# Output projection and the MLP's opening in a hybrid decoder step: matmuls in traced order, norm steps at set units

## The chip, the core and the metric

The kernel runs on one core of one Trainium2 chip. Times are microseconds of device time. The engines are TensorE (PE; its weight loads are PEld), VectorE (DVE), ScalarE (ACT), GpSimd (POOL) and SyncE (SP, which here only issues DMAs). The metric is the time of one execution, the median of several.

## What is computed

One decoder layer for 1024 prompt tokens and 8 single-token samples, 1032 token columns in all, model width 1024, MLP width 2816. The part that the change touches:

```python
def rms_norm(x, g):
    xf = x.astype(jnp.float32)
    y = xf * lax.rsqrt(jnp.mean(xf * xf, axis=-1, keepdims=True) + EPS)
    return (y * g.astype(jnp.float32)).astype(x.dtype)

def conv_ffn(h, buf, w_in, conv_w, conv_b, w_out):
    z = jnp.einsum('btd,df->btf', h, w_in)
    g, u = jnp.split(z, [D_FF], axis=-1)
    xp = jnp.concatenate([buf.astype(g.dtype), g], axis=1)
    c = sum(conv_w[j] * xp[:, j:j + T] for j in range(CONV_W)) + conv_b
    y = jnp.einsum('btf,fd->btd', jax.nn.gelu(c) * u, w_out)
    return y, xp[:, -(CONV_W - 1):]
...
xp = xp + rms_norm(mix_out(ro, rg, do, subln_g[l], lam_i, w_o[l]), norm_mix_post[l])
h = rms_norm(xp, norm_ffn_pre[l])
f, cbuf = conv_ffn(h, ..., w_ffn_in[l], conv_w[l], conv_b[l], w_ffn_out[l])
xp = xp + rms_norm(f, norm_ffn_post[l])
```

Everything is in fp32.

## The kernel before

**Tiling.** Activations lie transposed: 128 channels on the partitions, tokens along the free axis, in three segments s = 0, 1, 2 of 344 tokens (the samples are the last 8 columns of s = 2). An fp32 product is made of three matmuls of rounded parts: high weight by high row, high by low, low by high (`prod3`, lines 112 to 117). High parts are ScalarE copies, low parts VectorE subtractions (`split_w`, line 102). A *unit* is one `prod3` over all eight k: 24 matmuls into one PSUM bank. There are eight banks: two tagged mm, three S, two t, one o.

**Output projection** (line 878). For each s, eight blocks d of 128 output channels. For d = 0, 1 and s = 0, 1 seven of the eight k were multiplied earlier (`first`, line 794), beside the last retention head; only three matmuls are left there. After a unit ScalarE copies the bank, scaled, into `mix` (eight buffers) and squares it into `sq`; POOL adds the squares into `acc`.

**The two norms** (`norms_stage`, line 830) are a generator, one per segment, which the projection and the MLP's opening step forward with `next(chain)`. `rstd_1` sums `acc` over the channels with six small matmuls into `n1` (called n in the rows), then VectorE (`ms`), POOL (`rr`, a power) and VectorE (`rs`, six `dg`) turn it into diagonal matrices; `rstd_2` spreads the factor over the partitions with two matmuls into `bc`. Then the residual is added (`x1`, one buffer, loaded by SP), its squares go into `acc2`, it is stored by ScalarE's queue, and `rstd_1` and `rstd_2` come again; last, `ht` = x1 * gain * bc is split into `hh` and `hl`.

**The MLP's opening** (`ffn_in`, line 921). Blocks j = 0, 1 of the gate and up weights are multiplied directly: for j, s in (0,0), (0,1), (1,0), (1,1) a gate unit (`gp`) and an up unit (`up`) each, then, after line 1006, s = 2 for both j. Each ends with a chain of ScalarE and VectorE steps (convolution, gelu, product) and a store to `ad` or `ad2`.

**Token sums** (line 991). From j = 2 on the segments 0 and 1 are multiplied in Strassen's manner (`block`, line 1056; seven products of half size instead of eight): for each k in 0..3 POOL forms combinations of rows of `hh` + `hl`, and `put` splits them into `tw[0..2]` and over `hh[1]`, `hl[1]`. The first product that reads them is `pb` with `tw[0]` (line 1070).

**Order.** A planner orders the instructions of every engine by its own estimate of when each is ready, and gives buffers as they come free; the order is fixed before the launch, and each engine works through its queue in that order. Under `tc.manual_schedule(engines={PE})` TensorE's instructions keep the order in which they were traced; in the kernel before this holds for the blocks j = 2 to 21 only (lines 1119 to 1126).

**The y stage** (line 1198). `load_t` brings weights and rows by SP's queue; `finish` (line 1135) is a generator that ends a part: factor, then per row of 128 channels a VectorE product, a POOL add into `x1` and a store to `yT` by SP's queue.

Of the kernel before, what the change touches and what calls it, by code (L numbers as in the profile page):

```python
# [18 lines left out]
P = 128  # L19
# [7 lines left out]
ND = D // P  # L27
# [24 lines left out]
def step_kernel(ctx: ExitStack, tc: tile.TileContext, gam, g128, xT, w_in, w_o, w_f, w_y, norms, ngb, cst, subln,  # L52
# [777 lines left out]
    def norms_stage(s, acc, mix):  # L830

        yield
        dg = rstd_1(pw, acc)
        yield
# [5 lines left out]
        for d in range(ND):  # L840
            nc.vector.tensor_tensor(mix[d], mix[d], bc, ALU.mult)
            (nc.vector if d % 2 else nc.gpsimd).tensor_tensor(x1[:, d, :], x1[:, d, :], mix[d], ALU.add)
            add_sq(pw, acc2, x1[:, d, :], d == 0, nc.vector)
            if d % 2:
                yield
        nc.scalar.dma_start(x1d[:, :, s * SEG:(s + 1) * SEG], x1)
        yield
        yield
        yield
        dg = rstd_1(pw, acc2)  # L850
        yield
# [4 lines left out]
        if s == 0:  # L856
            zt = pw.tile([P, ND, 2], F32, name="zt")
            nc.gpsimd.memset(zt, 0.0)
            nc.vector.tensor_copy(a[:, :, 0:2], zt)
            nc.vector.tensor_copy(b[:, :, 0:2], zt)  # L860
        else:
            nc.vector.tensor_copy(a[:, :, 0:2], hh[-1][:, :, SEG:SEG + 2].bitcast(F32))
            nc.vector.tensor_copy(b[:, :, 0:2], hl[-1][:, :, SEG:SEG + 2].bitcast(F32))
        for d in range(ND):
            t = pw.tile([P, SEG], F32, tag="sq", bufs=3, name="ht")
            nc.vector.scalar_tensor_tensor(t, x1[:, d, :], gn[:, 2, d:d + 1], bc, ALU.mult, ALU.mult)
            nc.scalar.activation(a[:, d, 2:SEG + 2], t, AF.Copy)
            nc.vector.tensor_tensor(b[:, d, 2:SEG + 2], t, a[:, d, 2:SEG + 2].bitcast(F32), ALU.subtract)
            if d % 2 and d < ND - 1:
                yield  # L870
        hh.append(a)
        hl.append(b)
        yield

    chain = None
    rot = 0
    w_all = [*w2, split_w(load_w(w_o[2]), wo, "o", bufs=6)]
    for s in range(3):
# [3 lines left out]
        for d in range(ND):  # L882
# [3 lines left out]
            else:  # L886
# [3 lines left out]
                ps = bank(("mm", "S", "S", "mm", "S")[rot % 5], "ps_o")[:, 0:SEG]  # L890
                rot += 1
# [4 lines left out]
            add_sq(pw, acc, ps, d == 0, nc.gpsimd)  # L896
            if chain is not None and (d, s) not in first:
                next(chain, None)
                next(chain, None)
        if chain is not None:  # L900
            for _ in chain:
                pass
        chain = norms_stage(s, acc, mix)
# [64 lines left out]
    for j in range(2):  # L968
        for s in range(2):
            for _ in ffn_in(j, s, *wj[j]):  # L970
                next(chain, None)
                next(chain, None)
    for _ in chain:
        pass
    closed(pw_cm)
# [8 lines left out]
    def part(t, s, k):  # L984
        return t[s][:, k, 2:SEG + 2].bitcast(F32)

# [4 lines left out]
    for k in range(4):  # L991
        b12, b22, t1, t2, t3 = (tt.tile([P, SEG], F32, tag=f"tt{i}", name=f"tt{i}") for i in range(5))
        G = nc.gpsimd.tensor_tensor
        G(b12, part(hh, 1, k), part(hl, 1, k), ALU.add)
        G(b22, part(hh, 1, 4 + k), part(hl, 1, 4 + k), ALU.add)
        G(t3, b22, b12, ALU.subtract)
        put(tw[1][:, 0, k], tw[1][:, 1, k], t3)
        G(t1, b12, part(hh, 0, k), ALU.subtract)
        G(t1, t1, part(hl, 0, k), ALU.subtract)
        G(t2, b22, t1, ALU.subtract)  # L1000
        put(tw[0][:, 0, k], tw[0][:, 1, k], t2)
        G(b12, part(hh, 0, 4 + k), t2, ALU.subtract)
        G(b12, b12, part(hl, 0, 4 + k), ALU.add)
        put(tw[2][:, 0, k], tw[2][:, 1, k], b12)
        put(hh[1][:, k, 2:SEG + 2], hl[1][:, k, 2:SEG + 2], t1)
    closed(t_cm)

# [111 lines left out]
    fixed = tc.manual_schedule(engines={mybir.EngineType.PE})  # L1119
    fixed.__enter__()  # L1120
# [14 lines left out]
    def finish(part, acc, fv, x1):  # L1135
# [6 lines left out]
        for d in range(ND):  # L1142
            nc.vector.tensor_tensor(fv[:, d, :], fv[:, d, :], bs, ALU.mult)
            nc.gpsimd.tensor_tensor(x1[:, d, :], x1[:, d, :], fv[:, d, :], ALU.add)
            nc.sync.dma_start(yT[part, :, d, :], x1[:, d, :])
            yield
# [256 lines left out]
```

## Time and profile before

| | |
|---|---|
| median of 3 runs | 1396.34 us (1395.2 to 1397.21) |
| the profiled execution | 1393.19 us |
| its span, first to last instruction | 1391.1 us |
| PE busy | 1317.4 us, 95% of the span |
| VectorE busy | 980.6 us, 70% |
| ScalarE busy | 574.4 us, 41% |
| POOL busy | 494.7 us, 36% |
| chain of work that ended last | PE 66%, VectorE 16%, POOL 7%, DMA 5%, issue 4%, ScalarE 2% |

The profiled execution is one run of the program; all durations come from it. "Idle before" in a row is the time for which the engine stood still before that instruction, with the instruction that released it. The ends of matmuls are modelled: neighbouring matmuls overlap in the rows, and the distance between two starts is what one costs. The granted clock is a share of TensorE's full speed.

### The profile page before, as it was taken

How to read it: one execution, taken by the hardware profiler on the slowest of the kernel's cores; microseconds unless marked ns; L12 is line 12 of the kernel's file. 1: busy time of each engine (PE TensorE's matmuls, PEld its weight loads, DVE VectorE, ACT ScalarE, POOL GpSimd, SP SyncE). 2: the span in 40 equal slices, each digit the busy share in tenths (PEclk: the TensorE clock that was granted, in tenths of full speed). 3: DMA queues.
4: the chain of work that ended last, by engine and by line, in shares of the span. 5: the costliest groups of instructions: out<-in, count | busy, mean ns of one | idle time of the engine just before them, and what ended most of it. 6: DMA issues, size and time to landing. Idle time of an engine off the chain costs nothing.

```text
span 1391.1 us, 22792 instructions
## 1 busy us (share of the span) xinstructions
PE 1317.4 (95%) x8235; PEld 1270.0 (91%) x8235; DVE 980.6 (70%) x1832; ACT 574.4 (41%) x1148; POOL 494.7 (36%) x402
## 2 busy tenths in 40 slices
PE   6999989999999999998879999999999999989998
PEld 5999888888999999998879999999999999989976
DVE  7665759879688865478777777777777655565575
ACT  6254425335222145354344443443443345536544
POOL 5300356745545621444652332332432200140140
PEclk9999999999999999999989999999999999999999
DMA  5334275764564534233022222121122277667674
GB/s 220 118 102 134 85 238 195 218 202 126 163 192 142 176 120 160 71 113 109 29 92 79 81 97 74 69 91 68 70 91 69 84 259 261 211 210 251 188 235 156
DMA packets 96915, 196.51 MB, mean 141 GB/s; under 512 B 17306, under 2 KB 47130, under 8 KB 96418
## 3 DMA queue, kind: packets, MB, share of 16 engines
q1 hardware_dynamic: 90082, 183.45, 40.6%
q10 hardware_dynamic: 6720, 11.62, 2.3%
q8 instruction: 64, 1.05, 0.3%
q14 instruction: 49, 0.40, 0.1%
HBM read 155.11 MB, written 30.48 MB: 133 GB/s over the span
## 4 chain that ended last, share of the span: by engine, by line
PE 66%; DVE 16%; POOL 7%; DMA 5%; issue 4%; ACT 2%; SPq 0%; DVEq 0%; POOLq 0%; ACTq 0%
PE ps_y L1213 4%; PE ps_in L114 4%; PE ps_y L1212 4%; PE ps_y L1214 4%; PE ps_in L116 4%; PE ps_in L115 4%; DVE acc_v L587 3%; PE pb L1021 3%; PE pb L1020 3%; PE pb L1022 3%; PE up L1022 2%; PE pc L1021 2%; PE pc L1022 2%; PE up L1021 2%; PE pc L1020 2%
## 5 line engine op out<-in xcount | busy, mean ns | idle before, releaser
L114 PE MATMUL ps_in<-xh,wh 128*128 128x344 f32 x672 | 224.8, 335 | 6.8 <-ACT xh L193 5.9
L115 PE MATMUL ps_in<-xl,wh 128*128 128x344 f32 x672 | 221.2, 329 | 1.9 <-DVE xl L194 1.9
L116 PE MATMUL ps_in<-xh,wl 128*128 128x344 f32 x672 | 220.0, 327 | 1.1 <-DVE wl L109 1.1
L114 PEld LDWEIGHTS ps_in<-xh,wh 128*128 128x128 f32 x672 | 130.2, 194 | 9.9 <-ACT xh L193 5.9
L1153 DVE TENSOR_TENSOR wyl<-wyraw,wyh 128x1024 fp32r<-128x1024 f32 x66 | 83.7, 1271 | 74.1 <-ACT wyh L1152 71.8
L115 PEld LDWEIGHTS ps_in<-xl,wh 128*128 128x128 f32 x672 | 130.1, 194 | 4.4 <-DVE xl L194 3.6
L161 POOL TENSOR_TENSOR acc<-acc,sq 128x344 f32<-128x344 f32 (+1 forms) x56 | 59.0, 1054 | 208.8 <-ACT sq L160 203.9
L116 PEld LDWEIGHTS ps_in<-xh,wl 128*128 128x128 f32 x672 | 130.0, 193 | 1.6 <-DVE wl L109 1.4
L1212 PE MATMUL ps_y<-ah,wyh 128*128 128x388 f32 x352 | 120.2, 341 | 4.4 <-ACT ah L1163 4.4
L1039 POOL TENSOR_TENSOR S<-wraw 128x512 f32<-128x512 f32 x20 | 33.0, 1652 | 252.3 <-DMA wraw<-in_w_f 237.8
L1213 PE MATMUL ps_y<-al,wyh 128*128 128x388 f32 x352 | 120.1, 341 | 1.2 <-DVE al L1164 1.2
L1214 PE MATMUL ps_y<-ah,wyl 128*128 128x388 f32 x352 | 119.6, 340 | 0.0
L494 POOL TENSOR_TENSOR pg<-pg,qb 128x512 f32<-128x512 f32 x64 | 91.2, 1447 | 37.5 <-DMA pg<-in_kpool 26.9
L1152 ACT ACTIVATE wyh<-wyraw 128x1024 fp32r<-128x1024 f32 x66 | 69.7, 1058 | 73.8 <-PE ps_y L1213 43.5
L989 DVE TENSOR_TENSOR ww<-S,ww 128x512 fp32r<-128x512 f32 x80 | 88.6, 1125 | 9.1 <-ACT ww L988 9.1
L988 ACT ACTIVATE ww<-S 128x512 fp32r<-128x512 f32 x80 | 50.6, 634 | 94.2 <-POOL S L1040 33.9
L989 DVE TENSOR_TENSOR ww<-wraw,ww 128x512 fp32r<-128x512 f32 x80 | 75.2, 941 | 19.2 <-ACT ww L988 17.6
L1020 PE MATMUL pb<-tw,ww 128*128 128x344 f32 x240 | 77.3, 322 | 10.9 <-ACT tw L988 10.2
L988 ACT ACTIVATE ww<-wraw 128x512 fp32r<-128x512 f32 x80 | 50.1, 627 | 86.8 <-PE up L1022 63.4
L1164 DVE TENSOR_TENSOR al<-ar,ah 128x388 fp32r<-128x388 f32 (+2 forms) x110 | 60.5, 564 | 25.8 <-ACT ah L1163 24.9
L1021 PE MATMUL pb<-tw,ww 128*128 128x344 f32 x240 | 77.3, 322 | 0.8 <-DVE tw L989 0.8
L1022 PE MATMUL pb<-tw,ww 128*128 128x344 f32 x240 | 76.9, 321 | 0.0
(324 smaller groups left out, 3841.6 us busy)
## 6 DMA issues: line engine op xcount, KB each, us to landing
wyraw<-in_w_y SPq DMA_DIRECT2D x66, 512.0 KB, 3.8
wraw<-in_w_f SPq DMA_DIRECT2D x44, 512.0 KB, 3.2
pg<-in_kpool SPq DMA_DIRECT2D x64, 256.0 KB, 3.0
pg<-in_vpool SPq DMA_DIRECT2D x64, 256.0 KB, 2.7
wraw<-in_w_in SPq DMA_DIRECT2D x27, 512.0 KB, 4.1
ar<-ad SPq DMA_DIRECT2D x44, 194.0 KB, 3.8
ad<-cc SPq DMA_DIRECT2D x20, 344.0 KB, 2.3
ar<-ad SPq DMA_DIRECT2D x44, 150.0 KB, 3.3
```

The source lines that it names most:

```text
L114: nc.tensor.matmul(ps, lhsT=wh[:, k, :], rhs=ah[:, k, n0:n1], start=(first and i == 0), stop=False)
L115: nc.tensor.matmul(ps, lhsT=wh[:, k, :], rhs=al[:, k, n0:n1], start=False, stop=False)
L116: nc.tensor.matmul(ps, lhsT=wl[:, k, :], rhs=ah[:, k, n0:n1], start=False, stop=(last and i == len(order) - 1))
L494: nc.gpsimd.tensor_tensor(kp, kp, qb.rearrange("p (a b) -> p a b", b=P), ALU.mult)
L988: nc.scalar.activation(hi, t, AF.Copy)
L989: nc.vector.tensor_tensor(lo, t, hi.bitcast(F32), ALU.subtract)
L1020: nc.tensor.matmul(ps, lhsT=w[:, 0, k], rhs=bh, start=(first and k == 0), stop=False, skip_group_check=True)
L1021: nc.tensor.matmul(ps, lhsT=w[:, 0, k], rhs=bl, start=False, stop=False, skip_group_check=True)
L1022: nc.tensor.matmul(ps, lhsT=w[:, 1, k], rhs=bh, start=False, stop=(last and k == 3), skip_group_check=True)
L1212: nc.tensor.matmul(pss[d], lhsT=wh[:, i, w], rhs=ah, start=(f == 0), stop=False)
L1213: nc.tensor.matmul(pss[d], lhsT=wh[:, i, w], rhs=al, start=False, stop=False)
L1214: nc.tensor.matmul(pss[d], lhsT=wl[:, i, w], rhs=ah, start=False, stop=(f == NF - 1))
```

## The change

Five things are done.

1. TensorE's traced order begins before the output projection instead of before block 2, and holds to the end of the blocks. The banks of the projection's twenty whole units are given by a list (`tags`).
2. `norms_stage` has fewer yields: ten. The chains are no longer stepped twice after each unit and drained at the end of a segment; `unit_done` steps every chain after a unit by a number that `STEPS` holds for the count of units since the chain began. What is left is drained after (1,1).
3. Squares (`sq`) have two buffers instead of three; `ht` has a tag of its own with two, and for s = 1 eight kept rows, `h1`.
4. The token sums are formed from `h1` instead of from `hh[1]` + `hl[1]`: six POOL operations per k instead of eight, in another order and with more buffers (t1 four, the others two). The pool `pw` is closed after them.
5. In `finish` row d - 2 is stored after row d has been added; the last two rows are stored at the end.

```diff
     def norms_stage(s, acc, mix):
 
-        yield
         dg = rstd_1(pw, acc)
-        yield
         yield
         bc = rstd_2(dg)
         x1 = pw.tile([P, ND, SEG], F32, tag="x1", name="x1")
...
             (nc.vector if d % 2 else nc.gpsimd).tensor_tensor(x1[:, d, :], x1[:, d, :], mix[d], ALU.add)
-            add_sq(pw, acc2, x1[:, d, :], d == 0, nc.vector)
-            if d % 2:
+            add_sq(pw, acc2, x1[:, d, :], d == 0, nc.vector, bufs=2)
+            if d % 2 and d < ND - 1:
                 yield
         nc.scalar.dma_start(x1d[:, :, s * SEG:(s + 1) * SEG], x1)
         yield
-        yield
-        yield
         dg = rstd_1(pw, acc2)
-        yield
         yield
         bc = rstd_2(dg)
...
+        hh.append(a)
+        hl.append(b)
         for d in range(ND):
-            t = pw.tile([P, SEG], F32, tag="sq", bufs=3, name="ht")
+            if s == 1:
+                t = pw.tile([P, SEG], F32, tag="h1", bufs=8, name="h1")
+                h1.append(t)
+            else:
+                t = pw.tile([P, SEG], F32, tag="ht", bufs=2, name="ht")
             nc.vector.scalar_tensor_tensor(t, x1[:, d, :], gn[:, 2, d:d + 1], bc, ALU.mult, ALU.mult)
             nc.scalar.activation(a[:, d, 2:SEG + 2], t, AF.Copy)
             nc.vector.tensor_tensor(b[:, d, 2:SEG + 2], t, a[:, d, 2:SEG + 2].bitcast(F32), ALU.subtract)
-            if d % 2 and d < ND - 1:
+            if d % 2:
                 yield
-        hh.append(a)
-        hl.append(b)
-        yield
-
-    chain = None
+
+    h1 = []
+    STEPS = {0: 1, 2: 2, 3: 2, 5: 2, 7: 2, 8: 2}
+    chains = []
+
+    def unit_done():
+
+        for ch in list(chains):
+            for _ in range(STEPS.get(ch[1], 0)):
+                next(ch[0], None)
+            ch[1] += 1
+
+    fixed = tc.manual_schedule(engines={mybir.EngineType.PE})
+    fixed.__enter__()
+    tags = iter(("S", "o", "mm", "mm", "S", "o", "mm", "o", "mm", "S", "S", "S",
+                 "mm", "o", "mm", "S", "S", "S", "mm", "o"))
...
-                ps = bank(("mm", "S", "S", "mm", "S")[rot % 5], "ps_o")[:, 0:SEG]
-                rot += 1
+                ps = bank(next(tags), "ps_o")[:, 0:SEG]
                 prod3(ps, *w, mh, ml, order, 0, SEG)
...
-            add_sq(pw, acc, ps, d == 0, nc.gpsimd)
-            if chain is not None and (d, s) not in first:
-                next(chain, None)
-                next(chain, None)
-        if chain is not None:
-            for _ in chain:
-                pass
-        chain = norms_stage(s, acc, mix)
+            add_sq(pw, acc, ps, d == 0, nc.gpsimd, bufs=2)
+            if (d, s) not in first:
+                unit_done()
+        chains.append([norms_stage(s, acc, mix), 0])
...
     for j in range(2):
         for s in range(2):
             for _ in ffn_in(j, s, *wj[j]):
-                next(chain, None)
-                next(chain, None)
-    for _ in chain:
-        pass
-    closed(pw_cm)
+                unit_done()
+    for ch in chains:
+        for _ in ch[0]:
+            pass
...
     for k in range(4):
-        b12, b22, t1, t2, t3 = (tt.tile([P, SEG], F32, tag=f"tt{i}", name=f"tt{i}") for i in range(5))
+        t1, t2, t3, t4 = (tt.tile([P, SEG], F32, tag=f"tt{i}", bufs=(4 if i == 0 else 2), name=f"tt{i}")
+                          for i in range(4))
         G = nc.gpsimd.tensor_tensor
-        G(b12, part(hh, 1, k), part(hl, 1, k), ALU.add)
-        G(b22, part(hh, 1, 4 + k), part(hl, 1, 4 + k), ALU.add)
-        G(t3, b22, b12, ALU.subtract)
+        G(t1, h1[k], hh[0][:, k, 2:SEG + 2].bitcast(F32), ALU.subtract)
+        G(t1, t1, hl[0][:, k, 2:SEG + 2].bitcast(F32), ALU.subtract)
+        G(t2, h1[4 + k], t1, ALU.subtract)
+        put(tw[0][:, 0, k], tw[0][:, 1, k], t2)
+        G(t3, h1[4 + k], h1[k], ALU.subtract)
         put(tw[1][:, 0, k], tw[1][:, 1, k], t3)
-        G(t1, b12, part(hh, 0, k), ALU.subtract)
-        G(t1, t1, part(hl, 0, k), ALU.subtract)
-        G(t2, b22, t1, ALU.subtract)
-        put(tw[0][:, 0, k], tw[0][:, 1, k], t2)
-        G(b12, part(hh, 0, 4 + k), t2, ALU.subtract)
-        G(b12, b12, part(hl, 0, 4 + k), ALU.add)
-        put(tw[2][:, 0, k], tw[2][:, 1, k], b12)
+        G(t4, hh[0][:, 4 + k, 2:SEG + 2].bitcast(F32), t2, ALU.subtract)
+        G(t4, t4, hl[0][:, 4 + k, 2:SEG + 2].bitcast(F32), ALU.add)
+        put(tw[2][:, 0, k], tw[2][:, 1, k], t4)
         put(hh[1][:, k, 2:SEG + 2], hl[1][:, k, 2:SEG + 2], t1)
     closed(t_cm)
+    closed(pw_cm)
...
     src = sums(load_j(3))
-    fixed = tc.manual_schedule(engines={mybir.EngineType.PE})
-    fixed.__enter__()
     for j in range(2, NF):
...
             nc.gpsimd.tensor_tensor(x1[:, d, :], x1[:, d, :], fv[:, d, :], ALU.add)
+            if d > 1:
+                nc.sync.dma_start(yT[part, :, d - 2, :], x1[:, d - 2, :])
+            yield
+        for d in (ND - 2, ND - 1):
             nc.sync.dma_start(yT[part, :, d, :], x1[:, d, :])
-            yield
```

## Rows read from the trace of the kernel before

**Rows 1.** PE's waits, 495 to 720 us: total us, times, longest

```profile
PE pb L1020 <- ACT tw L988: 10.2, 2, 8.3
PE bc L146 <- DVE dg L138: 9.1, 5, 4.6
PE gp L1020 <- DVE c L938: 1.3, 1, 1.3
...
PE pb L1020 <- DVE u L1081: 0.7, 1, 0.7
```

**Rows 2.** stretches: PE, PEld, DVE, ACT, POOL busy (count), clock, DMA, GB/s

```profile
646.00:648.00 2.00, 1.70 (x8) 1.70 (x9) 1.99 (x9) 0.08 (x1) 0.47 (x1) 0.75 0.03 8
...
708.00:710.00 2.00, 2.00 (x13) 2.00 (x12) 1.31 (x3) 0.97 (x2) 0.00 (x0) 0.89 0.78 237
```

**Rows 3.** waits of all engines, 495 us to the end, one of POOL

```profile
POOL tt L998 <- DVE hl L989: 10.7, 1, 10.7
```

**Rows 4.** one stretch of 14 us within the projection, columns as above

```profile
578.00:592.00 14.00, 14.00 (x91) 14.00 (x90) 7.56 (x13) 7.63 (x19) 7.78 (x8) 1.00 0.28 102
```

**Rows 5.** PE in order of time, n and bc: start, length, line [idle before]

```profile
570.96 0.66 PE L127 MATMUL n<-ct,acc 128*128 128x1 f32 x6
...
574.26 0.55 PE L146 MATMUL bc<-dg,ones_r 128*128 128x344 f32 x2 [0.80 <-DVE dg L138]
...
592.61 0.66 PE L127 MATMUL n<-ct,acc 128*128 128x1 f32 x6
...
596.54 0.60 PE L146 MATMUL bc<-dg,ones_r 128*128 128x344 f32 x2 [1.41 <-DVE dg L138]
...
608.10 0.47 PE L146 MATMUL bc<-dg,ones_r 128*128 128x344 f32 x2
...
622.58 0.66 PE L127 MATMUL n<-ct,acc 128*128 128x1 f32 x6
...
627.18 0.60 PE L146 MATMUL bc<-dg,ones_r 128*128 128x344 f32 x2 [2.10 <-DVE dg L138]
...
633.90 0.76 PE L127 MATMUL n<-ct,acc 128*128 128x1 f32 x6 [0.23 <-POOL acc L161]
...
646.30 0.60 PE L146 MATMUL bc<-dg,ones_r 128*128 128x344 f32 x2 [4.57 <-DVE dg L138]
...
660.30 0.66 PE L127 MATMUL n<-ct,acc 128*128 128x1 f32 x6
...
665.13 0.60 PE L146 MATMUL bc<-dg,ones_r 128*128 128x344 f32 x2 [0.27 <-DVE dg L138]
```

**Rows 6.** VectorE in order of time: each chain's last adds of squares

```profile
584.04 4.62 DVE L161 TENSOR_TENSOR acc<-acc,sq 128x344 f32<-128x344 f32 x6 [0.18 <-ACT sq L160]
...
618.18 2.92 DVE L161 TENSOR_TENSOR acc<-acc,sq 128x344 f32<-128x344 f32 x4
...
658.68 0.51 DVE L161 TENSOR_TENSOR acc<-acc,sq 128x344 f32<-128x344 f32 x1
```

**Rows 7.** in time: fourth partial product begins; first weight tail

```profile
538.10 0.42 PE L114 MATMUL ps_o<-mh,wh 128*128 128x344 f32 x1
...
542.53 1.23 DVE L109 TENSOR_TENSOR wl<-wraw,wh 128x1024 fp32r<-128x1024 f32 x1 [0.38 <-ACT wh L108]
```

**Rows 8.** in order of time: a POOL add and a VectorE cast

```profile
594.38 0.92 POOL L161 TENSOR_TENSOR acc<-acc,sq 128x344 f32<-128x344 f32 x1
594.44 0.88 DVE L133 CAST rs<-rr 128x3 fp32r<-128x3 f32 x1 [0.97 <-POOL rr L131]
```

**Rows 9.** y stage in order of time: POOL, SP's queue, PE

```profile
1223.12 14.04 POOL L1144 TENSOR_TENSOR x1y<-x1y,fv 128x388 f32<-128x388 f32 x8 [4.07 <-DVE fv L1143]
...
1224.91 3.81 SPq L1145 DMA_DIRECT2D out_yT<-x1y  x2
...
1233.73 0.42 SPq L1177 DMA_DIRECT2D ar<-ae  x1
...
1236.71 0.44 PE L1212 MATMUL ps_y<-ah,wyh 128*128 128x388 f32 x1 [4.39 <-ACT ah L1163]
```

More of the change, by code (lines that the diff above doesn't have):

```diff
@@ L982, in step_kernel @@
     t_cm, tt = opened("tt")
-    def part(t, s, k):
-        return t[s][:, k, 2:SEG + 2].bitcast(F32)
     def put(hi, lo, t):
```

## The prediction

> **What bounds the kernel now.** First the page's busy times (the table above): TensorE (PE) is busy 95% of the span, so the change can pay only where PE stands still or runs slowly. I looked for those places with the view of ten-microsecond stretches over the whole span, then read the waits of PE in the stretches that the change touches, then the waiting instructions themselves in order of time, and the granted clock around them.
>
> In 495 to 720 us (the output projection, the MLP's opening, block j=2) PE is released late in eight groups of waits, 23.5 us in all, the first three of them in [rows 1], the other five under 1 us each. 10.2 us is `pb<-tw` waiting for ScalarE's copy of a combined token sum, in block j=2. 9.1 us is `bc<-dg`, the second half of a norm, waiting for VectorE. Each long stop is paid twice: after 646.3 the clock is 0.75, 0.50 and 0.90 of full in three stretches of 2 us (between the levels of 2.4 and 1.2 GHz), which loses 0.5 + 1.0 + 0.2 = 1.7 us; after 704 it is 0.50, 0.50 and 0.89, which loses 2.2 us ([rows 2] has the first and the last of these six). So 23.5 + 3.9 = **27.4 us** of these 225 are not work: 12.3 before block 2 (10.6 of stops, 1.7 of clock) and 15.1 in it (12.9 of stops, 2.2 of clock). From block 3 to the y stage PE has no stop, so what is won by the end of block 2 reaches the end.
>
> **Part by part.**
>
> *Token sums from kept rows.* Each of four k loses the two adds b12 and b22: 32 GpSimd (POOL) adds become 24, some 1 us each. More important is the order of buffers: in the old code POOL stood 10.7 us at L998, because the single t1 buffer is freed only when t1 has overwritten `hh[1]`, and that waits until PE has read `hh[1]` for the last time [rows 3]. Now t1 has four buffers, and no add stands behind that. The sums start, as before, when the w_o tiles under them are free, which is when the projection ends; after that PE has the eight units of j=0,1, s=0,1, then four of s=2, then 24 matmuls of block 2, before it reads tw[0]: 12 x 3.8 + 4 = 49 us. POOL needs 24 + 4 (chain 2's x1 adds) + 2 (rr) + 6 (the first weight sums), some 36 us. So the 10.2 and the small stops after it go. What is late next in block 2 is its bank for `gp`, which waited 1.3 us for VectorE [rows 1], and a sum that waited 0.7: ends 0 and 2.0, I take 1.0. **Block 2: 15.1 becomes 1.0, a gain of 14.1.** The change keeps fp32 rows only where VectorE makes them anyway; no instruction is added.
>
> *TensorE in program order, norm steps at units.* A unit is 24 matmuls; 14 us hold 91, so 0.158 each and 3.8 us a unit [rows 4]. Count the yields of the new generator: call 1 is `rstd_1` (n), call 2 `rstd_2` (bc) with rows 0,1, calls 3 to 5 the other rows, call 6 the second `rstd_1`, call 7 the second `rstd_2`. `STEPS` gives unit 0 call 1, unit 2 calls 2 and 3, unit 3 calls 4 and 5, and **unit 5 both call 6 and call 7**. So in each of three chains:
> - first norm: two units (7.6 us) lie between n and bc, more than the 3.3 to 4.8 us that n to bc takes where nothing else is in the way [rows 5]. Its old stops, 0.8 in chain 0 and 4.6 in chain 2, go.
> - second norm: n and bc stand next to each other, and nothing may overtake. PE waits the whole n-to-bc time less the 0.5 us of the six n matmuls themselves. The same norms took 3.93, 4.60 and 4.83 us in the old trace [rows 5], so 3.4 + 4.1 + 4.3 = **11.8 us**. The first norm of chain 0, on a quiet VectorE, took 3.30: three times that less 0.5 is 8.4, the low end. Before, 11 matmuls or more stood in between, and the stops were only 1.41, 2.10 and 0.27.
> - before that, n itself waits for the sum of squares. From bc to its last add took 14.4, 13.0 and 12.9 us (574.26 to 588.66, 608.10 to 621.10, 646.30 to 659.19) [rows 5, 6]; from call 2 at unit 2 to call 6 at unit 5 PE has bc and three units, 0.45 + 11.4 = 11.9. So 2.5 + 1.1 + 1.0 = **4.6 us**. Squares now share two buffers instead of three, between POOL's and VectorE's adds, which can lengthen this; the low end is 0, the high end twice the 4.6.
> - clock: each of these is 4.5 to 6 us with only six one-column matmuls inside. The old stop of 4.57 us dropped the clock and cost 1.7; one of 2.10 at 627 us did not [rows 5]. I take 1.7 three times, **5.1**; ends 0 and 5.1.
>
> At the start the order costs too: the third matmul of d=2, s=0 needs the weight tail that VectorE ends at 543.76, and PE is there at 542.8 (the fourth partial product begins at 538.10 and has 21 matmuls, 3.3 us; six closing matmuls take 1.0) [rows 7]: **1.0 us**, in place of the old 0.7 at 551.6 that is in the 12.3. Banks are given by hand; the tightest is S at d=6, s=1, which needs the square of d=0 some 3 us after bc, and PE comes 4.2 us after bc: nothing.
>
> hh[2] is read two units after its bc, and VectorE makes it in 16 steps of some 0.6 us, with PE reading the eight rows in turn over 3.8 us: nothing again, at most 2.
>
> Queues behind these waits: ScalarE's mix copies of s+1 wait for chain s's x1 adds, as now; SP's load of x1 for chain s+1 waits until chain s has made its last h row, and the w_f loads behind it have a unit of slack. The x1 store (call 5) stays on ScalarE's queue, behind no wait of PE's.
>
> **Opening before block 2: 1.0 + 4.6 + 11.8 + 5.1 = 22.5 in place of 12.3, a loss of 10.2.**
>
> The Trainium skill, page "SBUF — State Buffer", section "Who interferes with whom", says that VectorE's casts and tensor-with-scalar operations can need the port pair that it shares with GpSimd, and that whoever is second stands fully still. This trace agrees: the cast of rs took 0.88 us when a POOL add had started 0.06 us before it [rows 8], and the page speaks against this change in chain 2, whose dg now runs beside the token sums. By the page alone the quiet 8.4 would not be reached there.
>
> *y rows stored two rows later.* In the y stage PE stood 4.39 us at 1236.71, because an `ar` load stood in SP's queue behind y stores that wait for POOL's adds: eight of them in 14.04 us, 1.75 a row [rows 9]. If each store moved two rows back in the queue, the load would go 3.5 us earlier, and a loss of clock as after 646 (1.7) might go with it. But SP's order is not the traced one: the store at 1224.91 was traced behind loads that went at 1233 and later, so the planner issues a store when it thinks the row ready. Tracing it later does not change when the row is ready. I take 0; ends 0 and -5. The two last stores come at the chain's next call: nothing waits for them.
>
> **Sum.** 14.1 - 10.2 = 3.9 us off the profiled execution: 1393.19 - 3.9 = 1389.3. The median of the runs shown is 3.15 us above the profiled one, so the forecast is **1392.4 us**.
>
> **The rivals.**
> - *Covered* (faster): the squares are done in time and the clock holds. Then only 1.0 + 11.8 + 1.0 is left of 27.4, a gain of 13.6: 1382.7. For it: VectorE is busy only 70% of the span, so with PE in order it may run closer behind; a stop of 2.10 left the clock alone. Against it: 13 us in all three old chains, and a stop of 4.57 that did drop the clock. Chance 0.18.
> - *Stores do move* in SP's queue: the 3.9 and 5.2 more, 1387.2. Against it the order of the SP rows. Chance 0.13.
> - *VectorE's queue* (slower): an in-order PE now pays whatever stands ahead of dg in VectorE's fixed order. Chain 2's first norm took 12.4 us from n to bc (633.90 to 646.30) [rows 5], with h rows, a weight tail and a conv step ahead of dg in that queue. There 44 other matmuls covered most of it; at unit 5 nothing does. If chain 2's second norm, with conv steps and 16 remainders of token sums around it, takes as long, that is 12.4 - 4.8 = 7.6 more: 1400.0. It decides from the point at which the three second norms together stop PE for more than 11.8 + 3.9 = 15.7 us beyond the wait of n. For it: chain 2 at unit 5 is exactly such a place. Against it: with PE still, the other engines run out of work soon. Chance 0.21.
> - The forecast, 1387 to 1398, has the remaining 0.48.
>
> **How the numbers follow.** 0.2% (2.8 us) is about what can be told from no change: faster is below 1393.5, slower above 1399.1. The forecast's 0.48 lies at its faster side by 0.25, within by 0.20, beyond by 0.03. Faster: 0.18 + 0.12 + 0.25 = 0.55. Same: 0.20 + 0.01 + 0.01 = 0.22. Slower: 0.20 + 0.03 = 0.23. The range goes from the covered case to the first price of VectorE's queue with a little beyond it: 1382 to 1401; the forecast's own is 1387 to 1398.
>
> **What the changed profile would show.** Block 2 without a wait of `pb` for `tw` (first step); three pairs n, bc at unit 5 with a stop of 3.4 to 4.3 us between them and one of 1 to 2.5 us before (second); the clock at half after each (third); the first norms without a stop; the same order of stores and `ar` loads on SP with a stop of some 4 us near the old 1236 (fourth). Wrong would be: no drop of the clock, n that never waits, a bc that waits 8 us or more, or POOL still late for block 2.

## The result: 0.6% slower, and where the time went

| | before | after |
|---|---|---|
| median of six runs | 1397.28 us | 1404.24 us (1402.32 to 1409.73) |
| ratio, 95% interval | | 1.0059 (1.0038 to 1.0081) |
| the profiled execution | 1393.19 us | 1402.51 us |
| its span | 1391.1 us | 1400.5 us |

The change makes the kernel slower by 0.4 to 0.8%, where 0.3% faster was forecast. The two profiled executions differ by 9.4 us of span, and the difference can be cut at six instructions that both traces have:

| stretch | before | after | difference |
|---|---|---|---|
| to the last transpose of the heads, ahead of the changed code | 538.2 | 540.7 | +2.5 |
| "opening": from there to block 2's first product `pa` | 146.4 | 174.6 | +28.2 |
| block 2 | 37.8 | 20.9 | -16.9 |
| block 3 to the last block's last product | 396.8 | 396.8 | 0.0 |
| to the last `ps_y` | 196.8 | 194.0 | -2.8 |
| to the last `ps_n`, code that is the same | 69.0 | 67.3 | -1.7 |

So the changed places took 28.2 - 16.9 - 2.8 = 8.5 us more. The first thing to read is what TensorE (PE) waits for. This is its list of waits from 540 to 720 us in the trace of after (total us, times, longest us):

```profile
PE bc L146 <- DVE dg L138: 17.3, 5, 8.0
PE n L127 <- DVE acc L161: 13.0, 3, 6.7
PE ps_o L116 <- DVE wl L109: 1.1, 2, 0.7
PE gp L115 <- DVE hl L869: 0.3, 1, 0.3
```

Against [rows 1], `pb` no longer waits for `tw`: 10.2 of the 16.9 us that block 2 gained. Its smaller stops were 2.8 us and the lower clock beside them cost 2.8; some 1 us I can't place. But `bc` waits 17.3 us instead of 9.1, and `n`, which hardly waited before, 13.0. In order of time the stops are these (start, length, line, and in brackets the idle time before and who ended it):

```profile
597.03 0.73 PE L127 MATMUL n<-ct,acc 128*128 128x1 f32 x6 [2.83 <-DVE acc L161]
601.01 0.94 PE L146 MATMUL bc<-dg,ones_r 128*128 128x344 f32 x2 [3.25 <-DVE dg L138]
```

That is chain 0's second norm. Chain 1's has 6.66 and 3.25 (at 633.38 and 637.94), chain 2's 3.47 and 2.56 (at 685.88 and 689.26). And one that I had not forecast at all: chain 2's **first** broadcast, at 668.01, after 8.05 us, 16.4 us after its `n`. Each is paid a second time in the clock. Stretches of 4 us (columns as in [rows 2]):

```profile
600.00:604.00 4.00, 2.99 (x10) 2.99 (x11) 3.09 (x11) 0.98 (x2) 0.00 (x0) 0.50 0.01 2
...
636.00:640.00 4.00, 2.06 (x7) 2.06 (x8) 3.97 (x11) 0.29 (x1) 0.71 (x1) 0.50 0.02 4
...
664.00:668.00 4.00, 0.00 (x0) 0.00 (x0) 4.00 (x6) 0.85 (x3) 4.00 (x6) 0.50 0.00 0
...
688.00:692.00 4.00, 2.74 (x9) 2.74 (x10) 3.11 (x12) 0.97 (x2) 0.00 (x0) 0.50 0.39 140
```

Four times the granted clock stands at the lower level, 1.2 GHz, in or just after one of these stops. To compare kernels I use one sum, **not work**: over stretches of 2 us from 540 to 740, the time in which PE is not busy, plus its busy time times (1 - clock). It is 28.0 us before (23.5 idle, 4.5 clock) and 40.8 after (31.9 idle, 9.0 clock).

What made chain 2's first norm late is in the rows of GpSimd (POOL), ScalarE (ACT) and VectorE (DVE) between its `n` (651.62) and its `bc` (668.01):

```profile
654.54 0.92 POOL L1000 TENSOR_TENSOR tt<-h,tt 128x344 f32<-128x344 f32 x1
...
655.49 0.49 ACT L991 ACTIVATE tw<-tt 128x344 fp32r<-128x344 f32 x1 [2.31 <-POOL tt L1000]
...
656.17 1.20 POOL L1002 TENSOR_TENSOR tt<-h,h 128x344 f32<-128x344 f32 x1
657.34 1.20 POOL L1004 TENSOR_TENSOR tt<-hh,tt 128x344 f32<-128x344 f32 x1
...
660.40 0.79 POOL L999 TENSOR_TENSOR tt<-tt,hl 128x344 f32<-128x344 f32 x1
661.15 0.86 POOL L131 TENSOR_TENSOR rr<-ms,ct 128x3 f32<-128x3 f32 x1
```

```profile
656.01 0.57 DVE L992 TENSOR_TENSOR tw<-tt,tw 128x344 fp32r<-128x344 f32 x1 [2.10 <-ACT tw L991]
656.76 0.98 DVE L992 TENSOR_TENSOR tw<-tt,tw 128x344 fp32r<-128x344 f32 x1 [0.18 <-ACT tw L991]
657.67 0.15 DVE L129 TENSOR_SCALAR ms<-n 128x3 f32<-128x3 f32 x1
...
662.04 0.87 DVE L133 CAST rs<-rr 128x3 fp32r<-128x3 f32 x1 [3.13 <-POOL rr L131]
...
663.70 5.12 DVE L138 TENSOR_SCALAR dg<-ct,rs 128x128 fp32r<-128x128 f32 x6
```

`ms`, the first step of the norm, could run when the six `n` were done, at about 652.3, and ran at 657.67: ahead of it in VectorE's queue stand remainders of token sums (L992) that wait for ScalarE's copies, which wait for POOL's adds. Then `rr` waits until 661.15 behind POOL's adds, and the six `dg` take 5.12 us where the other five norms of this trace take 1.22. The sums start at 646.1, when the projection is nearly over and 5.5 us before chain 2's first `n`; from there to 668.8 POOL's rows stand back to back.

With the old sums (*order_only* below, same order of PE) the first adds start just as early, 5.5 us before `n` (650.87), and `ms` comes 5.1 us late there too. But after 659.44 the next add of a sum runs only at 689.18, held back by the single t1 buffer as in [rows 3], so `rr` and `dg` are hardly held up:

```profile
656.62 0.15 DVE L129 TENSOR_SCALAR ms<-n 128x3 f32<-128x3 f32 x1
...
657.66 0.86 POOL L131 TENSOR_TENSOR rr<-ms,ct 128x3 f32<-128x3 f32 x1
658.50 0.94 POOL L999 TENSOR_TENSOR tt<-tt,tt 128x344 f32<-128x344 f32 x1
...
659.92 1.21 DVE L138 TENSOR_SCALAR dg<-ct,rs 128x128 fp32r<-128x128 f32 x6
```

There `n` to `bc` takes 10.1 us, here 16.4.

The y stage: the order on SP's queue did change (start, time in the queue). First after, then a row of before.

```profile
1238.70 3.81 SPq L1147 DMA_DIRECT2D out_yT<-x1y  x2
1242.59 0.38 SPq L1180 DMA_DIRECT2D ar<-ad  x1
1243.03 0.44 SPq L1181 DMA_DIRECT2D ar<-ae  x1
...
1245.04 1.31 SPq L1147 DMA_DIRECT2D out_yT<-x1y  x2
```

```profile
1232.39 1.29 SPq L1145 DMA_DIRECT2D out_yT<-x1y  x2
```

Before, one `ar` load went between the two pairs of stores, and the second pair (at 1232.39) ahead of the load of 1233.73 [rows 9]; now four loads go between them, and PE's stop of 4.39 us is gone.

### The profile page after: what moved, and what is told of

Same layout as the page of the kernel before. It is cut to its first block, busy times and chain, and to the rows that moved or that the text cites. A ratio compares the mean times of both kernels' runs of the same rounds, so it can differ in the third digit from the quotient of the medians.

```text
span 1400.5 us, 22794 instructions
## 1 busy us (share of the span) xinstructions
PE 1320.4 (94%) x8235; PEld 1273.6 (91%) x8235; DVE 982.7 (70%) x1832; ACT 574.2 (41%) x1148; POOL 480.0 (34%) x394
## 3 DMA queue, kind: packets, MB, share of 16 engines
q8 instruction: 64, 1.05, 0.3%
## 4 chain that ended last, share of the span: by engine, by line
PE 47%; DVE 3%; POOL 2%; issue 1%; DMA 1%; ACT 1%; POOLq 0%; DVEq 0%; SPq 0%; ACTq 0%
PE ps_y L1217 4%; PE ps_y L1216 4%; PE ps_y L1218 4%; PE pb L1024 3%; PE pb L1025 3%; PE pb L1023 3%; PE gp L1023 2%; PE up L1025 2%; PE pc L1024 2%; PE pc L1025 2%; PE up L1024 2%; PE gp L1025 2%; PE pc L1023 2%; PE pa L1024 2%; PE pa L1023 2%; PE up L1023 2%
## 5 line engine op out<-in xcount | busy, mean ns | idle before, releaser
L1042 POOL TENSOR_TENSOR S<-wraw 128x512 f32<-128x512 f32 x20 | 31.2, 1560 | 264.0 <-DMA wraw<-in_w_f 249.6
L494 POOL TENSOR_TENSOR pg<-pg,qb 128x512 f32<-128x512 f32 x64 | 90.4, 1432 | 40.6 <-DMA pg<-in_kpool 29.1
L992 DVE TENSOR_TENSOR ww<-S,ww 128x512 fp32r<-128x512 f32 x80 | 87.0, 1105 | 9.0 <-ACT ww L991 9.0
L992 DVE TENSOR_TENSOR ww<-wraw,ww 128x512 fp32r<-128x512 f32 x80 | 75.2, 939 | 22.2 <-ACT ww L991 20.5
L108 ACT ACTIVATE wh<-wraw 128x1024 fp32r<-128x1024 f32 (+1 forms) x41 | 42.5, 1035 | 88.5 <-PE ps_in L115 44.6
L1024 PE MATMUL pb<-tw,ww 128*128 128x344 f32 x240 | 76.8, 320 | 0.0
L1025 PE MATMUL pb<-tw,ww 128*128 128x344 f32 x240 | 76.8, 320 | 0.0
## 6 DMA issues: line engine op xcount, KB each, us to landing
ar<-ad SPq DMA_DIRECT2D x44, 194.0 KB, 3.8
```

The source lines that it names most:

```text
L494: nc.gpsimd.tensor_tensor(kp, kp, qb.rearrange("p (a b) -> p a b", b=P), ALU.mult)
L992: nc.vector.tensor_tensor(lo, t, hi.bitcast(F32), ALU.subtract)
L1024: nc.tensor.matmul(ps, lhsT=w[:, 0, k], rhs=bl, start=False, stop=False, skip_group_check=True)
L1025: nc.tensor.matmul(ps, lhsT=w[:, 1, k], rhs=bh, start=False, stop=(last and k == 3), skip_group_check=True)
```

## The experiments

Each kernel computes the whole function. Ratios are against runs of the kernel before on the same chip; "opening", "block 2" and "not work" are worked out as above, in us.

| kernel | median us | ratio (95%) | opening | block 2 | not work |
|---|---|---|---|---|---|
| before | 1397.28 | 1 | 146.4 | 37.8 | 28.0 |
| after | 1404.24 | 1.0059 (1.0038-1.0081) | 174.6 | 20.9 | 40.8 |
| y_only | 1389.98 | 0.9965 (0.9945-0.9985) | 146.8 | 37.4 | 28.1 |
| sums_only | 1385.49 | 0.9931 (0.9916-0.9947) | 153.7 | 22.4 | 19.4 |
| order_only | 1416.97 | 1.0159 (1.0142-1.0176) | 168.2 | 34.7 | 48.1 |
| sums_y | 1384.42 | 0.9912 (0.9896-0.9928) | 153.8 | 22.3 | 19.5 |
| sums_late | 1404.10 | 1.0068 (1.0047-1.0088) | 175.6 | 20.9 | 42.2 |
| sums_held | 1411.49 | 1.0105 (1.0085-1.0125) | 168.5 | 34.2 | 48.2 |
| bc_apart | 1399.62 | 1.0023 (1.0009-1.0036) | 172.4 | 20.9 | 38.1 |
| x1_two | 1402.95 | 1.0044 (1.0025-1.0063) | 173.2 | 20.9 | 39.0 |
| steps_only | 1388.30 | 0.9924 (0.9900-0.9948) | 159.5 | 20.9 | 24.5 |
| all_held | 1393.71 | 0.9982 (0.9968-0.9995) | 151.5 | 34.8 | 31.2 |
| held_split | 1389.45 | 0.9931 (0.9906-0.9956) | 148.0 | 34.1 | 26.1 |
| held_two | 1384.57 | 0.9914 (0.9893-0.9934) | 150.7 | 29.1 | 23.5 |

**The three parts, each alone.** *y_only*: the kernel before, with this:

```diff
-            nc.sync.dma_start(yT[part, :, d, :], x1[:, d, :])
+            if d > 1:
+                nc.sync.dma_start(yT[part, :, d - 2, :], x1[:, d - 2, :])
             yield
+        for d in (ND - 2, ND - 1):
+            nc.sync.dma_start(yT[part, :, d, :], x1[:, d, :])
```

> The kernel before with only the y stores traced two rows later. Theory A (the stores hold SP's queue: in the trace of after the loads of ar for the next units are issued ahead of the store of rows 2 and 3, and the stop of 4.39 us at 1236.71 of before shrinks to 0.6 + 1.05): 3 to 4.5 us faster, about 1393. Theory B (the step of the prediction: a store is issued when its row is ready, wherever it is traced): no change, 1396 to 1398, and the stop of about 4.4 us stays.

Theory A, and a little more. The stop of 4 us is gone, and 0.60 and 1.06 stand there instead; the ratio means 4.9 us (2.1 to 7.7) less. From the last block to the last `ps_y` the trace took 192.8 us against 196.8.

*sums_only*: the kernel before, with the token sums of after, the eight kept rows, and their pool closed later; in short:

```diff
-            t = pw.tile([P, SEG], F32, tag="sq", bufs=3, name="ht")
+            if s == 1:
+                t = pw.tile([P, SEG], F32, tag="h1", bufs=8, name="h1")
+                h1.append(t)
+            else:
+                t = pw.tile([P, SEG], F32, tag="sq", bufs=3, name="ht")
...
-        G(b12, part(hh, 1, k), part(hl, 1, k), ALU.add)
...
+        G(t1, h1[k], hh[0][:, k, 2:SEG + 2].bitcast(F32), ALU.subtract)
```

> The kernel before with only the token sums taken from the kept rows (four buffers of t1, h1 kept); TensorE's order of projection and opening is the planner's as before, y stores as before. Theory A (the stop ahead of block 2 is the single t1 buffer and the ten adds a step): block 2's stops of 15.1 us and a clock drop go, opening as before: 14 to 16 us faster, about 1382. Theory B (sums that no longer wait for the second segment's high and low parts stand ahead of chain 2's norms on GpSimd and VectorE, whoever orders TensorE): the gain in block 2 is there, but 5 to 10 us come back as stops ahead of chain 2's products in the opening: 1387 to 1392.

Theory B in the trace (its "ten adds a step" are eight); the time, 1385.49, lies between the two. Block 2 takes 15.4 us less, but 7.3 come back in the opening, and the time falls by 9.6. In the opening chain 2's first broadcast waits 5.36 instead of 4.57 and its second 1.10 instead of 0.27, two stops of 0.46 and 0.81 appear at `gp` for rows that VectorE and ScalarE make late, and the clock falls once more (628 to 634).

*order_only*: after, with the old token sums and y stores:

```diff
-        G(t1, h1[k], hh[0][:, k, 2:SEG + 2].bitcast(F32), ALU.subtract)
...
+        G(b12, part(hh, 1, k), part(hl, 1, k), ALU.add)
...
-            if d > 1:
-                nc.sync.dma_start(yT[part, :, d - 2, :], x1[:, d - 2, :])
+            nc.sync.dma_start(yT[part, :, d, :], x1[:, d, :])
```

> The kernel after with the old token sums and the old y stores: TensorE in program order and norm steps at set units alone. Theory A (the order costs the second norms' stops, 22 us with what chain 0 and 1 waited for, and three clock drops; the 8.3 us at chain 2's first norm are the token sums' doing): opening 18 to 20 us longer than before instead of 28, block 2 stops about as before (12 to 15 us): 1412 to 1418, and no stop over 2 us at chain 2's first broadcast. Theory B (the order alone costs all 28 us): 1423 to 1427, with the stop of 8 us at chain 2's first broadcast.

Theory A, at its upper end (the opening is 21.8 us longer than before). The waits of PE from 540 to 735:

```profile
PE n L127 <- DVE acc L161: 11.6, 3, 7.7
PE bc L146 <- DVE dg L138: 10.8, 4, 3.3
PE gp L1023 <- DVE c L941: 10.8, 1, 10.8
```

`n` waits 2.83 and 7.72 us in chains 0 and 1, much as in after, so this is the order's own; in chain 2 it waits 1.05. The broadcasts are 3.25, 3.25 and 2.56 at the second norms and only 1.71 at chain 2's first: **the 8.05 us of after need the new sums**. The last line stands in block 2, which still takes 34.7 us with the old sums. The ratios of the three parts multiply to 1.0054, against 1.0059 for the whole change: they add up, two gains of 0.4 and 0.7% and one loss of 1.6%.

**When the sums run.** *sums_late*: after, with

```diff
-        t1, t2, t3, t4 = (tt.tile([P, SEG], F32, tag=f"tt{i}", bufs=(4 if i == 0 else 2), name=f"tt{i}")
-                          for i in range(4))
+        t1 = pw.tile([P, SEG], F32, tag="mix", bufs=8, name="tt0")
+        t2, t3, t4 = (tt.tile([P, SEG], F32, tag=f"tt{i}", bufs=2, name=f"tt{i}") for i in range(1, 4))
```

> The kernel after, but t1 of the token sums lives in the ring of eight mix rows, so that the sums that need t1 wait until chain 2's first mix rows are used up; order of TensorE and y stores as in after. Theory A (the sums' adds and remainders stand ahead of chain 2's first norm on GpSimd, ScalarE and VectorE): the stop of 8.05 us at its broadcast falls to about 2, with a clock drop of 1.7 less: 7 to 10 us faster than after, about 1395; block 2 still without a stop over 2 us. Theory B (the norm is late by itself): the stop stays at about 8 us, 1402 to 1406. Theory C (the sums now come too late): the stop goes to block 2's products of the sums, 5 to 10 us there, about 1404.

None of the three. The stop at chain 2's first broadcast is gone, as A says, but the time isn't: chain 2's second norm now waits 9.99 (`n`) and 4.97 (`bc`), 15.0 instead of 6.0. POOL's rows show why:

```profile
671.00 0.92 POOL L1000 TENSOR_TENSOR tt<-h,tt 128x344 f32<-128x344 f32 x1
...
676.38 0.91 POOL L999 TENSOR_TENSOR tt<-tt,hl 128x344 f32<-128x344 f32 x1
677.25 1.77 POOL L840 TENSOR_TENSOR x<-x,mix 128x344 f32<-128x344 f32 x2
```

The two x1 adds that complete the rows for the second sum of squares stand behind twelve adds of sums in a row. ScalarE's queue holds chain 2 up as well:

```profile
671.07 0.49 ACT L991 ACTIVATE tw<-tt 128x344 fp32r<-128x344 f32 x1 [3.08 <-POOL tt L1005]
671.47 0.48 ACT L160 ACTIVATE sq<-x 128x344 f32<-128x344 f32 x1
```

A square of chain 2 stands behind a copy of a sum that waits 3.08 us for POOL.

*sums_held* keeps all sums until chain 2's last row is written, by a copy of one column of it into the tiles of t1 and t3 first (t2 and t4 need t1 and t2), and does t1 and t2 of all four rows ahead of t3 and t4; in short:

```diff
+    last = hl[2][:, ND - 1, 2:3].bitcast(F32)
...
+        nc.vector.tensor_copy(T1[k][:, 0:1], last)
+        G(T1[k], h1[k], hh[0][:, k, 2:SEG + 2].bitcast(F32), ALU.subtract)
```

> The kernel after with the token sums held until the last low row of the third segment is written (each sum's tile gets a 128x1 copy from it first), t1 and t2 of all four rows ahead of t3 and t4; order of TensorE, norm steps and y stores as in after. Theory A (the sums in the queues of GpSimd, VectorE and ScalarE make chain 2 late; held back only half way the stop moved to its second norm, 9.99 + 4.97 us): chain 2's stops fall to those of the kernel with the old sums (1.7 at the first broadcast, 1.05 + 2.56 at the second norm), 8 to 11 us faster than after, about 1394, and block 2 has no stop over 3 us. Theory B (chain 2 is late in program order whatever the sums do): no change, 1402 to 1406. Theory C (held so long, the sums are late for block 2): 5 to 12 us of stops at block 2's products of the sums, 1400 to 1406.

Theory A's first half holds, and more: chain 2's stops are 0 at the first broadcast and 0.38 and 2.55 at the second norm. Theory C decides the time, but the stops are larger than it said (16.3 us, and 1411 instead of 1400 to 1406) and not at the products that I named:

```profile
PE gp L1029 <- DVE c L945: 9.8, 1, 9.8
...
PE pa L1029 <- DVE cpt L942: 6.5, 1, 6.5
```

Block 2 waits for banks whose last readers on VectorE (`cpt`, `c`) stand behind remainders of the sums, which wait for POOL. So the sums hurt whatever they are queued ahead of. These three runs and order_only show the mechanism: 24 adds on POOL with 16 casts and 16 remainders behind them, in queues that nothing can overtake.

*sums_y* puts the two parts that gain into the kernel before, and leaves PE's order to the planner.

> The kernel before with the token sums of after and the y stores of after, TensorE's order of projection and opening left to the planner. Theory A (the parts add up: -9.6 us for the sums, -4.9 us for the stores, as each alone ran): 1380 to 1382 where before is 1395. Theory B (the stores' gain was in part the run's own spread, about 2.8 us in the trace of after): 1383 to 1385.

Nearer to B: 12.3 us less, where the two gains together make 14.5; the intervals allow both. It beats before and after.

**What the order costs.** *bc_apart*: after, with

```diff
-    STEPS = {0: 1, 2: 2, 3: 2, 5: 2, 7: 2, 8: 2}
+    STEPS = {0: 1, 2: 2, 3: 2, 5: 1, 6: 2, 7: 2, 8: 2}
```

> The kernel after with one unit of products between the second norm's sum and its broadcast (the broadcast at unit 6, rows at 6, 7 and 8). Theory A (the broadcasts wait 3.25, 3.25 and 2.56 us only because nothing of TensorE is traced between sum and broadcast): these 9.1 us go and little comes back: 7 to 10 us faster than after, about 1396. Theory B (a broadcast one unit later makes the segment's rows late for the products that read them, and VectorE has no room): stops of about the same size at the opening's gp: 1402 to 1406.

Between the two. The three broadcasts don't wait any more (9.1 us gone), but `n` of chains 1 and 2 waits 9.23 and 6.38 instead of 6.66 and 3.47, so that much of it comes back: PE comes earlier to chain 1's `n`, but that starts at 634.06, no earlier than the 633.38 of after, because its squares are no earlier.

*x1_two*: after, with two buffers of x1 (the second segment's h rows overwrite their x1 rows in place, so that memory is the same).

```diff
-        x1 = pw.tile([P, ND, SEG], F32, tag="x1", name="x1")
+        x1 = pw.tile([P, ND, SEG], F32, tag="x1", bufs=2, name="x1")
```

> The kernel after with two buffers of x1 (the second segment's rows are kept in place in x1, so nothing else changes in size). Theory A (chain 1's squares are late because its load of x waits until chain 0 has read x1, issued 614.56 and landed by 621): chain 1's second sum waits 2 to 3 us instead of 6.66, a drop of the clock less at most: 3 to 6 us faster than after, about 1399. Theory B (they are late because VectorE comes to chain 1's mix rows only at 616 to 619, behind chain 0's rows): under 2 us, 1402 to 1405.

In the trace A: chain 1's load of x goes out at 547.13 instead of 614.56, and its `n` waits 3.19 instead of 6.66. In the time B: 1 to 2 us, with intervals that overlap. The opening is 1.4 us shorter; idle time fell by 4.3, but the clock took back 2.4 of it.

*steps_only*: after, with other places for the steps, and the two weight pairs of a segment done before the next segment:

```diff
-    STEPS = {0: 1, 2: 2, 3: 2, 5: 2, 7: 2, 8: 2}
+    STEPS = {0: 1, 1: 2, 2: 2, 5: 1, 6: 4}
...
-    for j in range(2):
-        for s in range(2):
+    for s in range(2):
+        for j in range(2):
```

> The kernel after with norm steps at units 0, 1, 2, 5 and 6 (a unit of products between each sum and its broadcast, all rows written at unit 6) and both weight pairs of a segment before the next segment; x1 single and the sums as in after. Theory A (the places of the steps cost the second norms' stops; the sums ahead of chain 2's first norm cost the rest): the six stops of the second norms (22 us) fall below 8, the stop at chain 2's first broadcast stays at 6 to 9 us: 1385 to 1392. Theory B (a chain takes 14 to 18 us from broadcast to last square whatever the steps say, so the stops only move, as they did when the broadcasts alone were set apart): 1397 to 1402.

Theory A: 16 us off after by the medians. The six stops of the second norms fall from 22.0 to 2.4 us (0.23, 0.38, 1.80 and three of nothing). Chain 2's first broadcast still waits 5.49, its `n` 3.33, and a new stop of 5.44 stands at chain 1's first broadcast. So most of what the order cost lies in the steps' places. Not all of it: the opening is still 5.7 us longer than in sums_y, where the planner orders PE.

**Both together.** *all_held* is after with the edits of steps_only, x1_two and sums_held:

```diff
-    STEPS = {0: 1, 2: 2, 3: 2, 5: 2, 7: 2, 8: 2}
+    STEPS = {0: 1, 1: 2, 2: 2, 5: 1, 6: 4}
...
+        x1 = pw.tile([P, ND, SEG], F32, tag="x1", bufs=2, name="x1")
...
+        nc.vector.tensor_copy(T1[k][:, 0:1], last)
```

> The kernel after with four things changed at once: the sums held as in the run beside this, x1 in two buffers with the second segment's rows kept in place in it, both weight pairs of a segment in the opening before the next segment, and norm steps at units 0, 1, 2, 5 and 6 with a unit between each sum and its broadcast. Theory A (program order costs nothing by itself; it costs what the steps' places and the sums make chain 1 and 2 late by): stops and low clock of projection, opening and block 2 fall from 40.8 us in after to 10 to 15: 1376 to 1382. Theory B (VectorE's and GpSimd's work for a chain, 14 to 18 us from broadcast to the last square, doesn't fit beside the products at any place of the steps): 25 us or more of stops stay, 1390 or above.

The opening does what A says: before block 2 only 7.5 us of stops (5.45 of it at chain 1's first broadcast). But stops of 6.51 and 9.73 us like those of sums_held stand at block 2's first product and in block 2, and the time is B's. *held_split* gives the sums three starting points, where POOL stood idle: t1 after chain 2's last x1 add, t2 after its second `dg`, t3 and t4 after its last row (24 adds in all; the 28 of theory B is a miscount). Against all_held:

```diff
-        nc.vector.tensor_copy(T1[k][:, 0:1], last)
+        nc.vector.tensor_copy(T1[k][:, 0:1], x1_2[:, ND - 2, 0:1])
...
+        nc.vector.tensor_copy(T2[k][:, 0:1], dg_2[:, 1, SEG - 1:SEG].bitcast(F32))
```

> As the run with everything held, but the token sums in three parts: the eight adds of t1 after chain 2's last sum on GpSimd (it stood idle from 650 to 671 there), the four of t2 after chain 2's second dg, t3 and t4 after its last low row. Theory A (the sums cost time only where they stand ahead of chain 2's norms or of the opening's last copies out of the banks): the opening keeps its 7 us of stops, and of the 16.2 us ahead of and in block 2 less than 5 stay: 1376 to 1382. Theory B (28 adds and 16 casts with 16 remainders don't fit between chain 2 and block 2 on GpSimd and VectorE at all): 8 us or more of stops stay, 1384 to 1392.

Theory B's time, 1389: block 2 still stops 2.29 and 7.93, with VectorE waiting at 686 and 690 (2.46 and 2.45 us) for casts of t4. *held_two* moves t4 up behind t2, t3 to the end, and steps rows d2 to d7 one unit later:

```diff
-    STEPS = {0: 1, 1: 2, 2: 2, 5: 1, 6: 4}
+    STEPS = {0: 1, 1: 2, 2: 2, 5: 1, 6: 1, 7: 3}
...
-        t3 = tt.tile([P, SEG], F32, tag="tt2", bufs=3, name="tt2")
+        t3 = pw.tile([P, SEG], F32, tag="ht", bufs=2, name="t3")
```

> As the run with the sums in three parts, with two differences: t4 follows t2 at once (GpSimd stood idle from 667 to 677 there) and t3 takes the ring of the third segment's rows, so that it comes last and still after them; and the rows d2 to d7 of a segment are stepped at unit 7 instead of 6, so that VectorE makes the next chain's dg ahead of them (it was spread over 601 to 608 there, stop 5.44 us). Theory A (what stops TensorE is the place of each helper in the queues, not their amount): the stops of 2.29 and 7.93 us at block 2 fall below 3 together, that of 5.44 us below 2: 1374 to 1380. Theory B (VectorE is full from 660 to 700, and the stops only change their place): 1385 to 1390, with 10 us or more of stops from 600 on.

Theory B, at its edge. The stop at chain 1's broadcast falls from 5.44 to 2.71 and block 2's to 5.01, but 2.61 and several small ones appear at the `gp` that reads hh[2]; the stops add up to 14.8 us from 600 on. With sums_y (1384.42) it has the lowest median, and it is better than before and after; the intervals of sums_y, steps_only, held_split and sums_only overlap with its own. So no run shows that an order fixed by hand gains anything over the planner's: sums_y leaves it alone. Whether an order exists in which opening and block 2 are both free of stops stays open: with the fixed order the shortest opening was 148.0 and the shortest block 2 20.9, but never in the same kernel.

## Why the prediction was wrong, step by step

*What bounds the kernel now*: right. The 27.4 us not worked in 495 to 720 are 28.0 by the count used here, and every gain came out of them or out of the y stage. (A matmul's 0.158 us is the distance between starts in the rows; 14 us over the 91 of [rows 4] would be 0.154, because 91 counts matmuls cut by the ends of the stretch. Nothing hangs on it.)

*Token sums, block 2 from 15.1 to 1.0*: right in block 2 itself (15.4 less alone, 16.9 less in after, no `pb` waiting for `tw`; I had counted the low clock only from 704, though it is at 0.69 in 694 to 696 and at 0.50 from there). The step that failed is the one that tested whether the sums fit: I counted POOL's work (36 us) against the 49 us until PE reads tw[0], and asked only whether the sums would be **late**. No step of the sum asked who stands behind them: chain 2's `ms`, `rr`, `dg`, x1 adds. The buffer that held most of the old sums back was gone, so they came early, without a break. Alone the sums gave 9.6 us, not 14.1.

*First norms, "their old stops go"*: wrong for chain 2, 8.05 + 0.21 us. Two units of products between `n` and `bc` cover 7.6 us, and I took 3.3 to 4.8 for the norm "where nothing else is in the way"; the same change had put the sums in the way. With the old sums it was 1.71.

*Second norms, 11.8 us between n and bc*: the mechanism was right, the size too large: 3.25 + 3.25 + 2.56 = 9.1, near my low end of 8.4. From `n` to `bc` the norms took 3.98, 4.56 and 3.38 us where I had 3.93, 4.60 and 4.83. Two things made the stops shorter. The six `n` matmuls, of which I took off 0.5, took 0.73, 1.31 and 0.82, most in chain 1, where the granted clock was at 0.50. And in chain 2 no add of POOL stood beside VectorE's steps: cast and `dg` took 0.17 and 1.22 there, 0.90 and 1.90 before.

*The wait of n, 4.6 us*: the term that was most under-sized. It was 2.83 + 6.66 + 3.47 = 13.0, above the high end of 9.2. I took the old chains' 12.9 to 14.4 us from broadcast to last square; they took 14.5, 18.4 and 17.7. For chain 1 half of it is the single x1 buffer (3.5 us by x1_two): its load of x went out at 614.56, when chain 0 had made its last row, a step that I named under the queues and did not price. For chain 2 it goes with the new sums: 1.05 with the old ones. What the two buffers of squares add, which I had named as well, no run separates.

*Clock, 5.1 us*: 9.0, in four drops of about 2.2 instead of three of 1.7; the fourth belongs to chain 2's first norm.

*The start, 1.0, and hh[2], 0 to 2*: 0.67 + 0.46 and 0.33. Right.

*y stores, 0*: wrong, and the rival "Stores do move" priced it well (5.2 against 4.9 alone; 2.8 in the trace of after). I had concluded from one store, issued before loads that were traced ahead of it, that the traced order doesn't matter. Tracing the stores two rows later did put the second pair behind four loads instead of one; why the planner orders them so is not shown.

*Sum*: opening +28.2 where I had +10.2, block 2 -16.9 where I had -14.1, y -2.8 where I had 0. The opening's error by its terms, in not work: `n` +8.4, chain 2's first broadcast +8.3, clock +3.9, second broadcasts -2.7. The rival "VectorE's queue" had the mechanism and nearly the price (7.6 against 8.3 us), but at chain 2's second norm; it came at the first, and the sums stood behind every part of it: 5.4 us until `ms`, 3.3 until `rr`, 3.9 in `dg`. My own sign of being wrong, a `bc` that waits 8 us or more, came with it. "Covered" fell: every one of the six waits came.

## What to carry to other kernels

When an edit takes away what held helper work back, look for what is next in the queues of the engines that do it, not only for whether it will be done in time: in queues that nothing overtakes, early work is an obstacle. When an order is fixed by hand, put work between a reduction and what needs its result, in every chain, and price the wait before the reduction by the loads and buffers of its own chain. Try the parts of a change apart: two of these three gained 1% together while the third lost 1.6%.

## What the runs showed of the hardware

Six `dg` of 128x128 took 5.12 us beside back-to-back POOL adds at 663.70, and 1.22 in the five other norms of the same trace; a cast of 128x3 took 0.87 instead of 0.17. The Trainium skill, page "SBUF — State Buffer", section "Who interferes with whom", says that whoever of VectorE and GpSimd comes second to their shared ports stands still for the other's whole instruction; 0.85 us for each `dg` is about the length of one add (0.78 to 0.92), and each of the six ends within 0.1 us of the end of an add, so this trace agrees.

The length of a stop doesn't tell whether the clock falls. A stop of 2.10 us at 627 left it at full in the trace of before [rows 5]; one of 2.09 at the same broadcast took it down in sums_only. A stretch of before, then two rows of sums_only (the stop and the stretch):

```profile
628.00:632.00 4.00, 4.00 (x27) 4.00 (x26) 4.00 (x8) 2.38 (x6) 1.93 (x2) 1.00 0.00 0
```

```profile
628.93 0.60 PE L146 MATMUL bc<-dg,ones_r 128*128 128x344 f32 x2 [2.09 <-DVE dg L138]
...
628.00:632.00 4.00, 3.06 (x13) 3.07 (x14) 3.54 (x11) 1.46 (x3) 1.81 (x4) 0.73 0.00 0
```

In the y stage the same small stops stand in y_only and in after (columns as in [rows 2]; first y_only):

```profile
1234.00:1238.00 4.00, 2.59 (x13) 2.18 (x13) 3.70 (x4) 0.90 (x4) 4.00 (x3) 1.00 0.86 252
1238.00:1242.00 4.00, 3.50 (x19) 2.94 (x18) 2.56 (x7) 2.08 (x5) 1.14 (x2) 1.00 1.04 340
```

```profile
1244.00:1248.00 4.00, 2.74 (x15) 2.10 (x13) 2.05 (x3) 2.08 (x5) 4.00 (x4) 1.00 0.77 207
1248.00:1252.00 4.00, 3.59 (x14) 3.59 (x15) 2.65 (x5) 1.12 (x2) 3.50 (x3) 0.70 0.92 293
```

PE was no busier in the first than in the second, and only the second lost clock, 1.7 us. What decides it stays open.
